# x and ctx transposed unscaled with 1/rms applied per K tile, column weights loaded in halves, first stage in a pinned order

## The chip, the cores and the metric

One core of one Trainium2 chip runs the kernel. The metric is device time in microseconds (us) of one execution. The kernel before takes 1290.29 us (median of three runs, 1290.16 to 1291.49).

## What is computed

One layer of a transformer block on 256 latent tokens (x) and 256 context tokens (ctx), model width 2048, everything in float32. The part that matters here is the beginning of it:

```
sh1, sc1 = first two of six parts of  silu(c) @ w_mod + b_mod          # for x
csh1, csc1 = the same of  silu(c_ctx) @ w_mod + b_mod                  # for ctx
h  = rmsnorm(x,   g_attn) * (1 + sc1)  + sh1
hc = rmsnorm(ctx, g_attn) * (1 + csc1) + csh1
cq, ckv, kr, qn, kn, vn, f = split(h @ w_in);  the same of hc @ w_in
```

Three head groups (latent attention, neighbourhood attention, Fourier mixing), an output projection, and a gated feed-forward with a convolution follow. rmsnorm divides each token's row by its root mean square (rms) and multiplies by a gain.

## The kernel before, in words

Every matrix product is made of three products in float32r: each operand is split into a high part (limb) H, its value rounded to float32r, and a low limb L, the rest. `mm3` (lines 107 to 114) issues H*H, H*L and L*H, which the profile shows as lines 108, 109 and 110. `split` makes limbs: a CAST on ACT (line 119) and a subtraction on DVE (line 120).

The weights come as one stream of tiles in a fixed list, `order`, of 1 MB each (`raw`, line 169), issued on SP's queue; `take` splits quarters of them into limbs (`hl`), four quarters ahead. A raw tile lies in a pool of 16 buffers of 8 KB per partition, which x, the transposed xT, the normed hx and hc and others share.

The first stage runs from the start of the program to about 145 us. Its steps:

- x and ctx come as four tiles `x` of 128 tokens (line 288). ACT squares and sums each (line 295), DVE and POOL make 1/rms (lines 104 and 105), and DVE multiplies the whole tile by it in place (line 297). Then PE transposes it in 16 pieces of 128 columns, four to a PSUM bank (line 360), and DVE and ACT in turn copy the banks to xT (line 361). PE's transposes use the unit matrix `ident`, which is the first part of the packed constants `sm`, loaded by ACT's queue (line 291).
- Then a loop over 16 K tiles (128 rows of w_in each) with three kinds of work on PE. A column sum, `mod1_mm`: 32 matmuls over two raw tiles of w_mod (line 314) that give the shift and scale of this K tile, copied to SBUF by ACT as `part` (line 317). `mod1_h`: two transposes of `part` (line 322), three small DVE operations to `mt` (lines 326 to 328), and the normed K tile in limbs: DVE makes it in full (line 338), ACT its high limb hx or hc (line 339), DVE the low one (line 340). And `g1`: seven column groups of w_in times this K tile, 42 matmuls per K tile, accumulated in seven PSUM banks `g`. Their weights are the raw tiles A, one for two K tiles, split in four quarters: quarters 0 and 1 belong to the even K tile, 2 and 3 to the odd one.

In the code the column sum of K tile g stands ahead of four products of K tile g-1, then `mod1_h` of g, then the other three products (`G1_CUT` is 4 of `N_A` = 7). A scheduler places the instructions of the five engines; each engine then works through its own list strictly in that order. After the loop the stage of the neighbourhood values (V) begins, and beside it columns of the late modulation parts are summed on DVE from tiles `wm`, loaded by POOL's queue (lines 217 and 232); their limbs `acl` are summed over partitions by PE (lines 266 and 267).

## Time and profile before

| what | value |
|---|---|
| median of three runs | 1290.29 us |
| span of the profiled execution | 1286.6 us |
| median less that span | 3.7 us |
| PE busy | 1251.4 us, 97% of the span |
| DVE busy | 982.8 us, 76% |
| ACT busy | 699.7 us, 54% |
| DMA, mean rate | 237 GB/s |
| end of the first stage (first product of V) | 144.92 us |

The span runs from the first to the last instruction; the 3.7 us are what the median of the runs has beside it (the profile gives no other time of its execution). Times below count from the span's start. PE is the engine that the kernel is built around: it has little idle time, so a stage is read by when PE begins, what it must do, and where it waits.

### The profile page before, as it was taken

The numbers are of one execution on the slowest core, as the hardware profiler recorded it, in microseconds if no ns is written. First come the engines' busy times: TensorE is split into PE (matmuls) and PEld (weight loads), VectorE is DVE, ScalarE is ACT, GpSimd is POOL, SyncE is SP. The second block draws the span as 40 slices with busy tenths as digits, with TensorE's granted clock in tenths as the row PEclk, the third lists the DMA queues.
The fourth block names the chain that finished last, engine by engine and source line by source line (L and its number), as shares of the span: only waits on it lengthen the run. The fifth ranks groups of instructions, "written<-read, shape, count | busy, mean of one in ns | idle before, by whom it ended". The sixth has DMA issues, their size and how long they took to land.

```text
span 1286.6 us, 22194 instructions
## 1 busy us (share of the span) xinstructions
PE 1251.4 (97%) x8688; PEld 1129.4 (88%) x8688; DVE 982.8 (76%) x1805; ACT 699.7 (54%) x1327; POOL 115.0 (9%) x177
## 2 busy tenths in 40 slices
PE   5999989999999999999999999999999999999996
PEld 4888869998887888999999788999988999899985
DVE  5444588999989788798988956778766778777785
ACT  5333323765555555576666544666654566456662
POOL 0000121111111013212111100000000000000000
PEclk9999989999999999999999999999999999999998
DMA  9998688776756977766666657544455645554521
GB/s 384 419 404 317 233 291 313 239 251 240 246 196 250 363 279 293 306 255 236 227 229 230 229 196 290 184 149 164 169 192 209 243 141 193 190 207 160 189 107 66
DMA packets 53657, 304.96 MB, mean 237 GB/s; under 512 B 6064, under 2 KB 7216, under 8 KB 26800
## 3 DMA queue, kind: packets, MB, share of 16 engines
q1 hardware_dynamic: 34256, 234.37, 48.8%
q0 software_dynamic: 18432, 67.12, 15.2%
q10 hardware_dynamic: 864, 2.05, 0.4%
q8 instruction: 68, 1.11, 0.3%
q14 instruction: 37, 0.30, 0.1%
HBM read 301.42 MB, written 2.10 MB: 236 GB/s over the span
## 4 chain that ended last, share of the span: by engine, by line
PE 92%; DMA 3%; DVE 2%; ACT 1%; issue 1%; POOL 0%; DVEq 0%; POOLq 0%; ACTq 0%
PE ps L108 27%; PE ps L110 26%; PE ps L109 26%; PE g L108 2%; PE ms L314 2%; DMA wm<-in_wm_dram 2%; PE g L109 2%; PE g L110 2%; PE ps L489 1%; PE ps L360 1%; DMA sm<-in_small_dram 1%; DVE acc L232 1%; DVE hl L120 1%; PE ps L256 1%; ACT hl L119 0%
## 5 line engine op out<-in xcount | busy, mean ns | idle before, releaser
L119 ACT CAST hl<-raw 128x512 fp32r<-128x512 f32 (+2 forms) x732 | 443.6, 610 | 397.6 <-PE ps L110 315.7
L120 DVE TENSOR_TENSOR hl<-raw,hl 128x512 fp32r<-128x512 f32 (+2 forms) x732 | 486.4, 676 | 161.1 <-ACT hl L119 155.7
L108 PE MATMUL ps<-h,hl 128*128 128x258 f32 x1408 | 398.5, 283 | 0.0
L109 PE MATMUL ps<-h,hl 128*128 128x258 f32 x1408 | 396.2, 281 | 0.0
L110 PE MATMUL ps<-h,hl 128*128 128x258 f32 x1408 | 395.8, 281 | 0.0
L109 PEld LDWEIGHTS ps<-h,hl 128*128 128x128 f32 x1408 | 266.5, 189 | 0.2
L110 PEld LDWEIGHTS ps<-h,hl 128*128 128x128 f32 x1408 | 265.8, 189 | 0.0
L108 PEld LDWEIGHTS ps<-h,hl 128*128 128x128 f32 x1408 | 265.4, 189 | 0.2
L232 DVE SCALAR_TENSOR_TENSOR acc<-wm,c,acc 128x1024 f32<-128x1024 f32 x120 | 153.3, 1277 | 8.4 <-DMA wm<-in_wm_dram 8.2
L108 PE MATMUL ps<-hl,act 128*128 128x512 f32 x344 | 135.1, 393 | 0.0
L109 PE MATMUL ps<-hl,act 128*128 128x512 f32 x344 | 135.0, 393 | 0.0
L110 PE MATMUL ps<-hl,act 128*128 128x512 f32 x344 | 134.8, 392 | 0.0
L217 POOL DMA_DIRECT2D wm<-in_wm_dram x128 | 68.3, 534 | 303.1 <-DVE acc L232 225.5
L110 PEld LDWEIGHTS ps<-hl,act 128*128 128x128 f32 x344 | 64.7, 188 | 14.6
L108 PEld LDWEIGHTS ps<-hl,act 128*128 128x128 f32 x344 | 64.6, 188 | 14.3
L109 PEld LDWEIGHTS ps<-hl,act 128*128 128x128 f32 x344 | 64.7, 188 | 14.1
L212 POOL COPY hold<-hl 128x1 f32<-128x1 f32 x36 | 37.3, 1037 | 278.0 <-DVE hl L120 275.5
L817 DVE SCALAR_TENSOR_TENSOR cv<-ps,sm,cv 128x255 f32<-128x255 f32 x88 | 42.1, 481 | 24.8 <-ACT cv L816 24.4
L105 POOL TENSOR_TENSOR r<-v,mhalf 128x1 f32<-128x1 f32 (+1 forms) x3 | 4.0, 1317 | 563.1 <-DVE v L104 563.1
L816 ACT ACTIVATE cv<-ps,sm 128x256 f32<-128x256 f32 x88 | 49.5, 566 | 2.6
L108 PE MATMUL ps<-hl,mix 128*128 128x512 f32 x128 | 50.5, 394 | 0.0
L109 PE MATMUL ps<-hl,mix 128*128 128x512 f32 x128 | 50.1, 391 | 0.0
(272 smaller groups left out, 1996.1 us busy)
## 6 DMA issues: line engine op xcount, KB each, us to landing
raw<-in_wup_dram SPq DMA_DIRECT2D x88, 1024.0 KB, 4.9
wm<-in_wm_dram POOLq DMA_DIRECT2D x128, 512.0 KB, 4.8
raw<-in_wdn_dram SPq DMA_DIRECT2D x44, 1024.0 KB, 4.8
raw<-in_wm_dram SPq DMA_DIRECT2D x32, 1024.0 KB, 14.5
raw<-in_wo_dram SPq DMA_DIRECT2D x16, 1024.0 KB, 8.3
raw<-in_wB_dram SPq DMA_DIRECT2D x10, 1024.0 KB, 7.9
raw<-in_wA_dram SPq DMA_DIRECT2D x8, 896.0 KB, 14.8
x<-in_x_dram SPq DMA_DIRECT2D x4, 1024.0 KB, 8.8
```

Of the source, the lines that this page charges most:

```text
L108: pe.matmul(ps, lH, rH, start=first, stop=False, skip_group_check=skip)
L109: pe.matmul(ps, lH, rL, start=False, stop=False, skip_group_check=skip)
L110: pe.matmul(ps, lL, rH, start=False, stop=last, skip_group_check=skip)
L119: act.copy(H, src)
L120: return dve.tensor_tensor(L, src, H.bitcast(F32), ALU.subtract).ins
L212: hold = pool.tensor_copy(tiny(1, "hold"), recent[0][:, 1, 0:1].bitcast(F32)).ins
L217: pool.dma_start(w, a["wm2"][blk * 16 + kt])
L232: dve.scalar_tensor_tensor(m2["a"], w, c1[:, kt : kt + 1], m2["a"], ALU.mult, ALU.add)
L256: pe.matmul(ps[:, 2 * j : 2 * j + 2], v[:, j * P : (j + 1) * P], ones[:, 0:2], start=True, stop=True)
L314: pe.matmul(ms[r : r + 32, 0:256], cs[:, 8 * q + k, :], w[:, k, :], start=(q == 0 and k < 4), stop=(q == 1 and k >= 4), tile_position=(0, r))
L816: act.activation(t, ps[:, :SEQ], AF.Identity, bias=c[:, 3:4], scale=c[:, 1:2])
L817: dve.scalar_tensor_tensor(t[:, 1:], ps[:, : SEQ - 1], c[:, 0:1], t[:, 1:], ALU.mult, ALU.add)
```

## The change

- x and ctx are loaded in halves of 1024 columns, and PE transposes them as they land, unscaled, with a unit matrix `idt` that POOL makes (so that it needn't wait for `sm`). DVE alone copies the banks. `sm` is issued behind them in the code, `rope` later.
- 1/rms of all 512 tokens is made at once; four diagonal blocks `dgx` of it and one matmul with ones spread it over the partitions (`rxb`), and DVE multiplies it into xT, 512 columns per K tile, one K tile ahead of use.
- Each A tile comes in halves of 448 KB (896 columns). The second half (quarters 2 and 3) is issued behind the next K tile's two raw tiles of w_mod.
- `G1_CUT` is 2, K tile 1 has an order of its own, and `tc.issue_after` holds the column sums and the transposes behind the last `g1` product issued ahead of them in the code, and the DVE multiplication behind the last one's h.

```diff
-N_A, G1_CUT = 7, 4
+N_A, G1_CUT = 7, 2
...
+    idt = const.tile([P, P], F32, name="idt")
+    pool.affine_select(idt, ones, [[1, P]], ALU.is_equal, 0.0, base=0, channel_multiplier=-1)
...
-            last_dma[0] = sync.dma_start(raw[:, :w], a[name][idx]).ins
+            if key[0] == "A":
+                sync.dma_start(raw[:, : w // 2], a[name][idx, :, : w // 2])
+                late_half.append((raw[:, w // 2 : w], a[name][idx, :, w // 2 :]))
+            else:
+                last_dma[0] = sync.dma_start(raw[:, :w], a[name][idx]).ins
+                if late_half and key[0] == "m" and key[2] == 1:
+                    sync.dma_start(*late_half.pop())
...
-        sync.dma_start(x_, (a["x"] if t < 2 else a["ctx"])[(t % 2) * P : (t % 2 + 1) * P, :])
+        for h in range(2):
+            sync.dma_start(x_[:, h * 1024 : (h + 1) * 1024],
+                           (a["x"] if t < 2 else a["ctx"])[(t % 2) * P : (t % 2 + 1) * P, h * 1024 : (h + 1) * 1024])
...
-        act.activation(junk, xt[t], AF.Square, accum_out=ssx[:, t : t + 1])
-        rstd(rx[:, t : t + 1], ssx[:, t : t + 1], D)
-        dve.tensor_scalar(xt[t], xt[t], rx[:, t : t + 1], None, ALU.mult)
...
+                pe.transpose(ps[:, k * P : (k + 1) * P], xt[t][:, kt * P : (kt + 1) * P], idt)
+            dve.tensor_copy(xT[m][:, :, t * P : (t + 1) * P], ps.rearrange("p (k q) -> p k q", k=4))
+    rstd(rx, ssx, D)
+    dgs = b2(s="dgx")
+    for t in range(4):
+        dve.tensor_scalar(dgs[:, t * P : (t + 1) * P], idt, rx[:, t : t + 1], None, ALU.mult)
+    ps = bank()
+    pe.matmul(ps, ones, dgs, start=True, stop=True)
+    rx_made = act.copy(rxb, ps).ins
...
+            if g:
+                held.enter_context(tc.issue_after(g1_last[-1]))
...
+            dve.tensor_tensor(xk, xk, rxb, ALU.mult)
...
+        if g == 1:
+            g1(0, range(0, 4))
+            sb = mod1_mm(1)
+            with tc.issue_after(rx_made):
+                act.dma_start(rope, a["rope"])
+                act.activation(c1, smv("c1"), AF.Silu)
+            g1(0, range(4, 5))
+            mod1_h(1, sb)
+            g1(0, range(5, N_A))
+            continue
```

PE's list at the start of the loop. `raw` are tiles of w_mod, `ms` the bank of the column sums, `part` the sums on their way to the transposes, `g` the products. Before:

```order
L314 MATMUL ms_118<-raw_222,cs 32x256 x8
L314 MATMUL ms_118<-raw_224,cs 32x256 x8
L322 MATMUL ms_118<-sm,part_254 128x128 x2
L314 MATMUL ms_118<-raw_228,cs 32x256 x8
L314 MATMUL ms_118<-raw_230,cs 32x256 x8
L322 MATMUL ms_118<-sm,part_294 128x128 x2
L314 MATMUL ms_118<-raw_232,cs 32x256 x8
L108 MATMUL g_0_34_215<-hx_262,hl_296 128x256
```

Two and a half column sums and two pairs of transposes stand ahead of the first product there. PE's list of the changed kernel, at the same place:

```order
L317 MATMUL ps_211<-dgx_206,ones_r 128x512
L338 MATMUL ms_214<-raw_222,cs 32x256 x8
L338 MATMUL ms_214<-raw_224,cs 32x256 x8
L349 MATMUL ms_214<-idt,part_255 128x128 x2
L110 MATMUL g_0_34_215<-hx_264,hl_274 128x256
L110 MATMUL g_1_35_216<-hx_264,hl_274 128x256
```

One column sum and one pair of transposes stand ahead of the first product now, and the matmul that spreads 1/rms stands ahead of all of them.

ACT's list at the same place. `raw_226` is the first A tile; `hl_296` to `hl_305` are its four quarters, `hx_262` and `hc_263` the high limbs of the first K tile. Before:

```order
L317 COPY part_254<-ms_118 128x256
L119 CAST hl_296<-raw_226 128x512
L119 CAST hl_299<-raw_226 128x384
L119 CAST hl_302<-raw_226 128x512
L119 CAST hl_305<-raw_226 128x384
L317 COPY part_294<-ms_118 128x256
L339 ACTIVATE hx_262<-xT_77,mt_258 128x256
L339 ACTIVATE hc_263<-xT_77,mt_258 128x256
```

In the changed kernel the same A tile is `raw_226`, quarters 0 and 1 of it are `hl_274` and `hl_277`, quarters 2 and 3, from the late half, `hl_280` and `hl_283`:

```order
L122 CAST hl_274<-raw_226 128x512
L122 CAST hl_277<-raw_226 128x384
L394 ACTIVATE c_77<-sm 128x16
L341 COPY part_255<-ms_214 128x256
L122 CAST hl_280<-raw_226 128x512
L122 CAST hl_283<-raw_226 128x384
L371 ACTIVATE hx_264<-xT_79,mt_259 128x256
L371 ACTIVATE hc_265<-xT_79,mt_259 128x256
```

The two casts of the late half still stand ahead of the first K tile's high limbs, while the tile that they read now comes in two transfers, the second behind two more raw tiles of w_mod.

ACT's list around K tiles 4 and 5 before (`part_636` is the sum of K tile 5, `hx_586` with `mt_582` the limb of K tile 4):

```order
L119 CAST hl_644<-raw_374 128x512
L317 COPY part_554<-ms_118 128x256
L119 CAST hl_647<-raw_374 128x384
L317 COPY part_636<-ms_118 128x256
L339 ACTIVATE hx_586<-xT_78,mt_582 128x256
L339 ACTIVATE hc_587<-xT_78,mt_582 128x256
```

The copy of the next K tile's sum stands ahead of this K tile's limbs there; the list before has this at K tiles 4, 8 and 12 alike. In the list of the changed kernel it stands so at K tile 12 alone (`part_1343` is the sum of K tile 13, `hx_1280` with `mt_1275` the limb of K tile 12):

```order
L341 COPY part_1259<-ms_214 128x256
L122 CAST hl_1351<-raw_1076 128x512
L122 CAST hl_1354<-raw_1076 128x384
L341 COPY part_1343<-ms_214 128x256
L371 ACTIVATE hx_1280<-xT_82,mt_1275 128x256
L371 ACTIVATE hc_1281<-xT_82,mt_1275 128x256
```

Two of the three places are gone. Behind the first stage the lists of all five engines are the same before and after.

## Rows read from the trace of the kernel before

**Rows 1.** Page: the span, and busy time, share and instructions of each engine.

```profile
span 1286.6 us, 22194 instructions
PE 1251.4 (97%) x8688; PEld 1129.4 (88%) x8688; DVE 982.8 (76%) x1805; ACT 699.7 (54%) x1327; POOL 115.0 (9%) x177
```

**Rows 2.** Windows: length, busy us (instructions) by engine, granted clock, DMA share, GB/s.

```profile
9.00:10.00 1.00, 0.00 (x0) 0.00 (x0) 0.00 (x0) 0.51 (x2) 0.00 (x0) 1.00 1.05 426
20.00:30.00 10.00, 8.15 (x104) 5.52 (x106) 7.49 (x18) 6.50 (x13) 0.00 (x0) 1.00 1.02 423
60.00:80.00 20.00, 19.93 (x198) 17.43 (x202) 8.66 (x27) 6.72 (x14) 0.00 (x0) 1.00 1.01 417
```

**Rows 3.** Timeline of SP's queue: start, us, line, output and input, count.

```profile
0.75 0.87 SPq L288 DMA_DIRECT2D x<-in_x_dram  x2
6.60 0.43 SPq L169 DMA_DIRECT2D raw<-in_wA_dram  x1
9.48 6.25 SPq L169 DMA_DIRECT2D raw<-in_wm_dram  x4
```

**Rows 4.** DMA issues from 6.5 to 7 and from 9 to 10 us: us to landing.

```profile
raw<-in_wA_dram SPq DMA_DIRECT2D x1, 896.0 KB, 15.5
...
raw<-in_wm_dram SPq DMA_DIRECT2D x1, 1024.0 KB, 15.1
```

**Rows 5.** Timeline of PE, 23 to 31 us, with idle time before and what ended it.

```profile
23.36 1.93 PE L314 MATMUL ms<-raw,cs 128*32 128x256 f32 x32
25.79 0.44 PE L322 MATMUL ms<-sm,part 128*128 128x128 f32 x2 [0.49 <-ACT part L317]
30.95 0.39 PE L108 MATMUL g<-hx,hl 128*128 128x256 f32 x1
```

**Rows 6.** Timeline of ACT, 25 to 30 us.

```profile
25.63 1.96 ACT L119 CAST hl<-raw 128x512 fp32r<-128x512 f32 x4
28.83 0.60 ACT L339 ACTIVATE hx<-xT,mt 128x256 fp32r<-128x256 f32 x1
```

**Rows 7.** Chain that ended last: column sums of K tiles 3, 7, 8, 9, 11 and 15.

```profile
42.52 1.86 PE ms L314 x32
72.67 1.86 PE ms L314 x32
79.91 1.86 PE ms L314 x32
87.15 1.91 PE ms L314 x32
102.89 1.86 PE ms L314 x32
132.75 1.86 PE ms L314 x32
```

**Rows 8.** Timeline of ACT at 89 us, with idle time before.

```profile
89.08 0.37 ACT L317 COPY part<-ms 128x256 f32<-128x256 f32 x1 [6.46 <-PE ms L314]
89.35 0.60 ACT L339 ACTIVATE hx<-xT,mt 128x256 fp32r<-128x256 f32 x1
```

**Rows 9.** Timeline of PE: first matmul of V, the two waits for acl.

```profile
144.92 0.39 PE L108 MATMUL ps<-hl,hx 128*128 128x512 f32 x1
183.46 0.80 PE L266 MATMUL ps<-acl,ones_r 128*128 128x512 f32 x1 [3.39 <-ACT acl L119]
730.05 0.51 PE L266 MATMUL ps<-acl,ones_r 128*128 128x512 f32 x1 [1.62 <-ACT acl L119]
```

**Rows 10.** Windows: granted clock (column before the last two) around the two waits.

```profile
182.00:184.00 2.00, 0.54 (x1) 0.29 (x1) 1.92 (x3) 1.22 (x3) 0.54 (x1) 0.66 0.95 365
186.00:188.00 2.00, 2.00 (x6) 1.55 (x5) 2.00 (x3) 0.00 (x0) 0.54 (x1) 0.50 0.60 178
188.00:190.00 2.00, 2.00 (x7) 1.52 (x7) 1.25 (x3) 0.62 (x1) 0.54 (x1) 0.63 0.63 234
190.00:192.00 2.00, 2.00 (x10) 1.65 (x9) 1.96 (x2) 0.19 (x1) 0.54 (x1) 1.00 0.70 234
728.00:730.00 2.00, 0.43 (x2) 0.00 (x0) 1.95 (x3) 0.63 (x2) 0.00 (x0) 1.00 0.00 0
```

**Rows 11.** Page: a costly group of DVE: busy, mean ns of one, idle before.

```profile
L120 DVE TENSOR_TENSOR hl<-raw,hl 128x512 fp32r<-128x512 f32 (+2 forms) x732 | 486.4, 676 | 161.1 <-ACT hl L119 155.7
```

More of the change, by code (lines that the diff above doesn't have):

```diff
@@ L109, in mm3 @@
         pe.matmul(ps, lH, rL, start=False, stop=False, skip_group_check=skip)
-        pe.matmul(ps, lL, rH, start=False, stop=last, skip_group_check=skip)
+        ins = pe.matmul(ps, lL, rH, start=False, stop=last, skip_group_check=skip).ins
         pace[1] += pace[0] * 3 * rH.shape[-1] * 0.427e-3
@@ L114, in mm3 @@
             fill()
+        return ins
     def split(H, L, src, scale=None):
@@ L141, in block_kernel @@
            "d": ("wdn", 2048)}
-    raws, hls = {}, {}
+    raws, hls, late_half = {}, {}, []
     recent, last_split, last_dma = [None], [None], [None]
@@ L287, in block_kernel @@
         x_ = b8([P, D], s="x")
-        sync.dma_start(x_, (a["x"] if t < 2 else a["ctx"])[(t % 2) * P : (t % 2 + 1) * P, :])
+        for h in range(2):
+            sync.dma_start(x_[:, h * 1024 : (h + 1) * 1024],
+                           (a["x"] if t < 2 else a["ctx"])[(t % 2) * P : (t % 2 + 1) * P, h * 1024 : (h + 1) * 1024])
         xt.append(x_)
-        if t == 0:
-            act.dma_start(sm, a["small"])
-    act.dma_start(rope, a["rope"])
+    act.dma_start(sm, a["small"])
+    rxb = b2(s="rxb")
     for t in range(4):
         junk = b8([P, D], s="junk")
-        act.activation(junk, xt[t], AF.Square, accum_out=ssx[:, t : t + 1])
-        rstd(rx[:, t : t + 1], ssx[:, t : t + 1], D)
-        dve.tensor_scalar(xt[t], xt[t], rx[:, t : t + 1], None, ALU.mult)
-    act.activation(c1, smv("c1"), AF.Silu)
+        sq_last = act.activation(junk, xt[t], AF.Square, accum_out=ssx[:, t : t + 1]).ins
+        for m in range(4):
+            ps = bank()
+            for k in range(4):
+                kt = 4 * m + k
+                pe.transpose(ps[:, k * P : (k + 1) * P], xt[t][:, kt * P : (kt + 1) * P], idt)
[4 more added lines that the diff above has]
+        dve.tensor_scalar(dgs[:, t * P : (t + 1) * P], idt, rx[:, t : t + 1], None, ALU.mult)
+    ps = bank()
+    pe.matmul(ps, ones, dgs, start=True, stop=True)
+    rx_made = act.copy(rxb, ps).ins
+    hmade, g1_last = [], []
     hx, hc = [None] * 4, [None] * 4
@@ L307, in mod1_mm @@
     def mod1_mm(g):
-        for q in range(2):
-            w = raw_tile(("m", g, q), 6)
-            w = w.rearrange("p (k n) -> p k n", k=8)
-            for k in range(8):
-                r = 32 * (k % 4)
-                pe.matmul(ms[r : r + 32, 0:256], cs[:, 8 * q + k, :], w[:, k, :], start=(q == 0 and k < 4),
-                          stop=(q == 1 and k >= 4), tile_position=(0, r))
+        with ExitStack() as held:
+            if g:
+                held.enter_context(tc.issue_after(g1_last[-1]))
+            for q in range(2):
+                w = raw_tile(("m", g, q), 6)
+                w = w.rearrange("p (k n) -> p k n", k=8)
+                for k in range(8):
+                    r = 32 * (k % 4)
+                    pe.matmul(ms[r : r + 32, 0:256], cs[:, 8 * q + k, :], w[:, k, :], start=(q == 0 and k < 4),
+                              stop=(q == 1 and k >= 4), tile_position=(0, r))
         sb = b1(s="part")
@@ L320, in mod1_h @@
     def mod1_h(kt, sb):
-        for s in range(2):
-            pe.transpose(ms[:, 256 + s * P : 256 + (s + 1) * P], sb[:, s * P : (s + 1) * P], ident)
+        with ExitStack() as held:
+            if kt:
+                held.enter_context(tc.issue_after(g1_last[-1]))
+            for s in range(2):
+                pe.transpose(ms[:, 256 + s * P : 256 + (s + 1) * P], sb[:, s * P : (s + 1) * P], idt)
         t = tiny(4, "mt")
@@ L329, in mod1_h @@
         m = kt // 4
+        xk = xT[m][:, kt % 4, :]
+        with ExitStack() as held:
+            if kt:
+                held.enter_context(tc.issue_after(hmade[-1]))
+            dve.tensor_tensor(xk, xk, rxb, ALU.mult)
         if hx[m] is None:
@@ L352, in g1 @@
             mm3(accs[i][:, :SEQ], lH, lL, *hsl(hx, kt), first=(kt == 0), last=(kt == KT - 1), skip=True)
-            mm3(accs[i][:, SEQ:], lH, lL, *hsl(hc, kt), first=False, last=(kt == KT - 1), skip=True)
-    for t in range(4):
-        for m in range(4):
-            ps = bank()
-            for k in range(4):
-                kt = 4 * m + k
-                pe.transpose(ps[:, k * P : (k + 1) * P], xt[t][:, kt * P : (kt + 1) * P], ident)
-            (act.copy if m % 2 else dve.tensor_copy)(xT[m][:, :, t * P : (t + 1) * P],
-                                                     ps.rearrange("p (k q) -> p k q", k=4))
+            g1_last.append(mm3(accs[i][:, SEQ:], lH, lL, *hsl(hc, kt), first=False, last=(kt == KT - 1), skip=True))
     accs = [bank(f"g1_{i}") for i in range(N_A)]
     for g in range(KT):
+        if g == 1:
[8 more added lines that the diff above has]
+            continue
         sb = mod1_mm(g)
```

2 lines of the change are left out of this document (1 added, 1 removed).

## The prediction

> **What bounds the kernel now.** I read the page first: PE is busy for 1251.4 of 1286.6 us [rows 1], so the time is what PE must do, plus the little it waits, plus when it begins. The change touches only the first stage, so the next views were of that stage. The windows show its DMA at a share of 1.01 to 1.05, some 420 GB/s, from the start to about 80 us [rows 2]: at first the loads set the pace. The timeline of PE shows when that ends: the first product of the loop comes at 30.95 us [rows 5], and from there PE is busy (19.93 of 20 us in the window from 60 us [rows 2]). The stage ends with the first matmul of V at 144.92 [rows 9]. So PE takes 144.92 - 30.95 = 114.0 us from the first product to the end of the stage, and this bounds the stage; the loads bound only what comes ahead of 30.95.
>
> The chain of waits shows how evenly the 114.0 us run. Column sums that follow each other undisturbed start 7.24 us apart (79.91 and 87.15 [rows 7]): one sum (1.86), one pair of transposes (0.44 [rows 5]) and 42 products. Four K tiles should take 28.96 us, but from 42.52 to 72.67 it is 30.15, from there to 102.89 it is 30.22, and to 132.75 it is 29.86 [rows 7]: 1.19, 1.26 and 0.90 too much, 3.35 together. The rows of ACT show why: the copy of the next sum stands ahead of this K tile's high limb on ACT and waits 6.46 us for PE, and the limb starts only behind it, at 89.35 [rows 8]; PE, which has by then run out of products, waits with it. That is the place of the lists at K tiles 4, 8 and 12.
>
> **The change, term by term.** All durations are from the profiled execution, span 1286.6; the median of the runs is 1290.29, so 3.7 lie outside the span, and I keep them.
>
> *When the first product can start.* The earlier transposes look like a gain of many us, since column sums began at 23.36 [rows 5] and depended on the scaling. But the first product needs the high limb of K tile 0 from ACT, and in the changed list ACT first casts the late half of the first A tile, which SP issues behind two more raw tiles of w_mod. When does it land? Before, the A tile was issued at 6.60 and landed 15.5 later, at 22.1; the raw tile behind it was issued at 9.48 and landed 15.1 later, at 24.6 [rows 3, 4]. So 1 MB takes 2.5 us of the stream. Ahead of the late half's end stands what stood ahead of 22.1, plus two raw tiles: 22.1 + 5.0 = 27.1. The 256 KB of `rope`, issued later now, may fall behind it, which takes off up to 0.6; I take 26.8. Then ACT needs two casts (half of 1.96, so 1.0) and the limb (0.60) [rows 6]: 28.4, and the first product at 28.5. Against 30.95 that is **-2.45** (bounds -2.75 and -2.15). Does something else end later? The second raw tile of w_mod lands 2.2 ahead of the A tile, at 19.3 without `rope`; a sum takes 1.93, or twice that at the low clock, the copy 0.4, the transposes 0.44 to 0.9, and the three small DVE operations some 0.6: 22.7 to 25.1. That is 2.7 us or more ahead of the 27.8 at which ACT is through with the casts. So the whole prologue (halves of x, unit matrix by POOL, one DVE copying instead of two engines, 1/rms at once, the spreading matmul) is covered by the late half, and gives and costs nothing; without that cover it would set the start.
>
> *What PE has done by then.* Before, 2.5 sums and two pairs of transposes were done at 30.95; now, by the list, one sum and one pair. PE has to make up 1.5 sums of 1.9 and one pair of 0.44 after its first product: **+3.3**. So the earlier start is more than paid back: PE stands idle, for want of the late half, while work that it used to do there waits behind the first product in its list.
>
> *The clock.* PE has nothing to do from the end of the transposes (22.7 to 25) to 28.5, 3.5 to 5.8 us. The nearest row is the wait of 3.39 us that ended at 183.46 [rows 9]: the granted clock fell to 0.50 in it, at 182.6 (0.66 over the window from 182 means 1.36 us of low clock) and came back at 189.5 (0.63 over the window from 188) [rows 10]. [...] A wait of 1.62 us left it at 1.00 [rows 9, 10]. The new gap is as long as the first one or longer, so I expect the low clock when the products begin, for 5 to 6 us: **+2.75** (bounds 0 and 3.4, half of the 6.8 us for which it was low there).
>
> *What the pinned order takes away.* All three late limbs are 3.35 us. In the changed list two are gone, the one at K tile 12 is left. **-3.35 and +1.2** (bounds of what is left: 0.90 and 1.26).
>
> *Edits at nothing.* The DVE multiplication of xT by 1/rms (512 columns; about 0.68 us, as the DVE subtractions over 512 columns take, most of whose group has that form [rows 11]) runs once per 7.24 us on a DVE that is busy 8.66 of 20 us [rows 2], and one K tile ahead of its use; if it came late it would hold the low limb by 0.7. With `G1_CUT` 2, five groups of products (3.5 us) and a sum (1.9) cover the way from the transposes to the next limbs, where three groups did before. The stage behind has the same lists on all engines, so a shift of the stage's end is carried to the end of the program one to one.
>
> The halves of A and x put four more transfers of x and one of A into SP's queue ahead of the late half. The rows show a queue that pays nothing per transfer: `sm`, x and w_mod of different sizes move at a share of 1.05 [rows 2]. The bounds are nothing and SP's own time per issue, 0.87 / 2 = 0.43 [rows 3], each, and I take nothing, since the transfers already queue ahead of their turn. [...]
>
> **Sum:** -2.45 + 3.3 + 2.75 - 3.35 + 1.2 = +1.45. Span 1288.05, and with 3.7 outside 1291.7.
>
> **Rivals.**
>
> *The clock does not fall, or is back when the products begin.* For it speaks that the record shows one fall only, in a wait for a DVE and ACT chain; against it that the new gap is longer. -2.75: 1289.0. [...]
>
> *The halves do cost queue time* (the one that ends slower). Place: SP's queue ahead of the late half. Price: five more transfers at up to 0.43 are 2.15, so the first product comes at 30.6 and the time is 1293.9. It decides from about 0.23 us per transfer on, where the sum passes +2.6. Against it: the share of 1.05.
>
> *The late half does not hold ACT.* If the first limb were not behind it, the limb would be ready at about 24.2, the gap would be under 2 us, and the sum would be -6.75 + 3.3 - 2.15 = -5.6: 1286.1. This is the change as it reads in words. The list of ACT speaks against it.
>
> *The wait at 183 shrinks.* The loads of `wm` and the weights of V share the queues there, and the stage's end moves against them. If the 3.39 us became the 1.62 of the second wait, the clock would stay up: -1.8 - 3.0 = -4.8, so 1286.9. Against it: everything in that stage starts from the same lists, relative to its own start.
>
> **How the numbers follow.** The forecast has 0.59 and, by its own bounds, 1290.0 to 1293.3; the clock rival 0.13, the queue 0.14, the late half that holds nobody 0.06, the shrinking wait 0.08. A measurement of this kernel can tell about 0.2% (2.6 us) from no change. Above 1292.9 lie the queue's 0.14 and 0.12 of the forecast: slower 0.26. Below 1287.7 lie the last two, 0.14. The rest, 0.60, is within 0.2%. For 8 in 10 the range leaves out the late-half rival, half of the shrinking wait and the upper half of the queue: 1287.0 to 1294.0.
>
> **What would show it.** In the profile after: transposes of x from about 5 us, with the first sum at 19 to 20; ACT waiting for a DMA of A ahead of its third cast, until 26.5 to 27.1; the first product at 28.5; a granted clock of 0.5 for some 5 us around 30; one limb late at K tile 12 and none at 4 and 8; V's first matmul at 146 to 147. A first product ahead of 26, or a full clock at 30, would make it wrong, and so would a second wait of PE in the loop that these lists don't show.

## The result, and the profile after

| | before | after |
|---|---|---|
| median of the runs beside each other | 1290.22 us (4 runs) | 1295.8 us (4 runs, 1294.8 to 1296.7) |
| ratio, 95% interval | | 1.0054 (1.0033 to 1.0074) |
| span of the profiled execution | 1286.6 us | 1293.5 us |
| first product of the loop | 30.95 | 30.30 |
| first matmul of V | 144.92 | 147.19 |

The changed kernel is slower by 5.6 us (by the medians), and 1295.8 lies above the range that was forecast, 1287.0 to 1294.0. In a second pair, side by side on one chip, the two stood at 1288.15 and 1298.11 (runs n_before and n_after below). The page of the kernel after, first lines, beside [rows 1]:

```profile
span 1293.5 us, 22221 instructions
PE 1263.5 (98%) x8690; PEld 1137.3 (88%) x8690; DVE 993.5 (77%) x1826; ACT 695.9 (54%) x1320; POOL 115.3 (9%) x175
```

PE is busy 12.1 us longer than before, for two records more. That is the first thing to see: the time didn't go into waits alone. The first stage first, by the steps of the prediction. SP's queue, beside [rows 3]:

```profile
0.80 2.12 SPq L298 DMA_DIRECT2D x<-in_x_dram  x4
2.96 3.24 SPq L298 DMA_DIRECT2D x<-in_ctx_dram  x4
7.39 0.85 SPq L176 DMA_DIRECT2D raw<-in_wm_dram  x2
8.86 0.33 SPq L173 DMA_DIRECT2D raw<-in_wA_dram  x1
10.12 2.94 SPq L176 DMA_DIRECT2D raw<-in_wm_dram  x2
13.95 0.33 SPq L178 DMA_DIRECT2D raw<-in_wA_dram  x1
```

The first A transfer goes out at 8.86, where it was 6.60 [rows 3]; eight transfers of x keep SP until 6.2 us, and w_mod starts at 7.39. The late half goes out at 13.95. ACT's timeline, beside [rows 6], shows when it was there:

```profile
28.71 1.03 ACT L122 CAST hl<-raw 128x512 fp32r<-128x512 f32 x2 [2.89 <-DMA raw<-in_wA_dram]
29.65 0.60 ACT L371 ACTIVATE hx<-xT,mt 128x256 fp32r<-128x256 f32 x1
```

ACT waits 2.89 us for the DMA until 28.71, and the high limb stands behind its two casts, as foreseen, but 1.9 us later than foreseen. Where the 1.9 us arose can be read from the landings: the first half of A, the late half and `rope`, issued at 8.86, 13.95 and 22.05, with the us from issue to landing in the last column:

```profile
raw<-in_wA_dram SPq DMA_DIRECT2D x1, 448.0 KB, 12.5
raw<-in_wA_dram SPq DMA_DIRECT2D x1, 448.0 KB, 14.7
rope<-in_rope_dram ACTq DMA_DIRECT2D x1, 256.0 KB, 7.4
```

The first half lands at 21.3, some 0.6 us later than the forecast's own figures put it (26.8 less 5.0 for two raw tiles and 1.1 for 448 KB). The late half lands 7.3 us behind it instead of 6.1. The forecast had let `rope` fall half behind the late half; it was under way beside it, and its 256 KB are 0.6 us of the stream by the same 2.5 us for 1 MB.

PE's timeline, beside [rows 5, 9]:

```profile
19.96 2.04 PE L317 MATMUL ps<-dgx,ones_r 128*128 128x512 f32 x2 [3.56 <-DVE dgx L315]
21.94 3.44 PE L338 MATMUL ms<-raw,cs 128*32 128x256 f32 x32
25.88 0.44 PE L349 MATMUL ms<-idt,part 128*128 128x128 f32 x2 [0.50 <-ACT part L341]
30.30 0.79 PE L110 MATMUL g<-hx,hl 128*128 128x256 f32 x2 [3.99 <-ACT hx L371]
147.19 0.39 PE L110 MATMUL ps<-hl,hx 128*128 128x512 f32 x1
185.12 0.52 PE L275 MATMUL ps<-acl,ones_r 128*128 128x512 f32 x1 [2.88 <-ACT acl L122]
733.17 0.50 PE L275 MATMUL ps<-acl,ones_r 128*128 128x512 f32 x1 [0.61 <-ACT acl L122]
```

PE waits 3.56 us for `dgx`, a wait that the prediction didn't name, and 3.99 us for hx. The first of the two doesn't hold the first product: DVE's last operation for `mt` is over at 26.98, and the limb's place on ACT, behind the casts of the late half, comes only at 29.65:

```profile
26.82 0.16 DVE L355 SCALAR_TENSOR_TENSOR mt<-mt,sa 128x2 f32<-128x2 f32 x1
```

The windows show what that did to the clock (columns: length, busy us and instructions by engine, granted clock, DMA share, GB/s), beside [rows 10]:

```profile
0.00:5.00 5.00, 0.00 (x0) 0.00 (x0) 0.67 (x3) 0.00 (x0) 0.48 (x5) 1.00 0.56 170
20.00:25.00 5.00, 5.00 (x34) 1.81 (x34) 1.76 (x3) 1.63 (x4) 0.00 (x0) 0.50 1.03 426
28.00:32.00 4.00, 1.70 (x7) 1.59 (x8) 2.19 (x5) 2.03 (x4) 0.00 (x0) 0.56 0.99 410
32.00:36.00 4.00, 4.00 (x27) 3.78 (x30) 0.34 (x1) 0.99 (x2) 0.00 (x0) 0.59 1.04 427
185.00:189.00 4.00, 3.68 (x9) 2.72 (x10) 3.92 (x8) 1.11 (x3) 0.76 (x2) 0.57 0.79 300
```

The granted clock is at 0.50 from 18.2 to 25.0 and from 28.4 to 35.3: the column sum takes 3.44 us instead of 1.93, and 18 of the first products, from 31.29 to 35.13, start 0.213 us apart, where 0.117 is the spacing at 1.00.

**Where the rest went.** How much later the same matmul comes than before, read from the two timelines of PE: -0.65 at the first product, +2.27 at V, +0.78 at 198 us, +1.08 at 222, +1.58 at 381, +2.92 at 559, +5.23 at 986, +7.30 at the last one of the down projection (1275.7 and 1283.0). So 1.5 us of V's shift are gone by 198 us, and from there to the end 6.5 us arise, steadily, where the lists of all engines are the same and no wait is new. The second wait for `acl` even gives 1.0 us back on the way: it is 0.61 us long in after and was 1.62 [rows 9], and the shift goes from +4.13 ahead of it to +3.13 behind it. Windows in the middle of the up and the down projection; before:

```profile
570.00:670.00 100.00, 100.00 (x836) 99.83 (x836) 90.09 (x178) 65.09 (x125) 19.37 (x26) 1.00 0.66 235
954.00:1000.00 46.00, 46.00 (x202) 37.67 (x202) 29.66 (x46) 20.58 (x34) 0.00 (x0) 1.00 0.59 215
```

and after:

```profile
570.00:670.00 100.00, 100.00 (x831) 99.83 (x830) 89.51 (x174) 64.77 (x126) 19.49 (x25) 1.00 0.64 229
954.00:1000.00 46.00, 46.00 (x200) 37.26 (x199) 29.26 (x45) 20.59 (x34) 0.00 (x0) 1.00 0.54 193
```

PE is busy throughout at a granted clock of 1.00 in both, and does 831 matmuls where it did 836. As a number for this I take the *spacing*: the mean time from the start of a matmul to the start of the next of the same product, from the records of the trace, without the steps that have a wait or other work between them. In the up projection (4224 matmuls of 258 columns) it is 119.40 ns before and 120.27 after; in the down projection (1032 of 512) 230.13 and 231.9; in the output projection (384) 228.1 and 231.8; in the first stage's products 116.9 and 117.8. 4224 x 0.87 + 1032 x 1.8 + 384 x 3.7 = 3.7 + 1.9 + 1.4 = 7.0 us. That accounts for most of the 7.5 us that came up behind 198 us, the 6.5 that are left and the 1.0 that the second wait gave back.

### The profile page after: what moved, and what is told of

Its sections match the earlier page's. It is cut to its first block, busy times and chain, and to the rows that moved or that the text cites. A ratio compares the mean times of both kernels' runs of the same rounds, so it can differ in the third digit from the quotient of the medians.

```text
span 1293.5 us, 22221 instructions
## 1 busy us (share of the span) xinstructions
PE 1263.5 (98%) x8690; PEld 1137.3 (88%) x8690; DVE 993.5 (77%) x1826; ACT 695.9 (54%) x1320; POOL 115.3 (9%) x175
## 4 chain that ended last, share of the span: by engine, by line
PE 92%; DMA 4%; DVE 1%; ACT 1%; issue 1%; POOL 0%; DVEq 0%; POOLq 0%; ACTq 0%
PE ps L110 27%; PE ps L112 27%; PE ps L111 27%; DMA wm<-in_wm_dram 2%; PE g L110 2%; PE ms L338 2%; PE g L111 2%; PE g L112 2%; DMA raw<-in_wA_dram 1%; PE ps L523 1%; DMA x<-in_ctx_dram 1%; DVE acc L241 1%; PE ps L265 1%; DMA sa<-in_small_a_dram 0%; PE ms L349 0%
```

## Experiments: the spacing

What differs behind the first stage, if not the lists? The chip, the addresses of the pools in SBUF, which of the sixteen 8-KiB buffers (tag `b8`) and which PSUM bank each tile gets, and PE's list, which has one float32 matmul more at the start. The pools hand out a buffer in the order in which buffers came back, and the changed first stage gives them back in another order, so that from `hx` on every tile of before has another buffer in after, one to one (5 is 2 there, 8 is 3, and so on). They stand 8256 bytes apart.

**n_before and n_after**: the two kernels unchanged, on one chip.

> The kernel before, unchanged. In the two profiles so far the first stage ends 2.27 us later after the change, but the last matmul comes 7.3 us later: from 228 to 1262 us the shift grows from 1.16 to 7.28, with equal lists and no new waits, since matmuls of the up projection follow each other in 120.55 ns instead of 119.72 (mean). Theory of the chip: the two profiles fell on chips or moments of different speed; then this one shows about 120.5 like the changed kernel in the same job, and the true difference of the kernels is some 1 us. Theory of the addresses: the changed kernel's tiles lie elsewhere in SBUF and PE reads them slower; then this one shows 119.7 again, and a ratio of 1.000.

> The changed kernel, unchanged, beside n_before on the same chip. Theory of the addresses: 120.5 ns and 5 to 6 us slower than before. Theory of the chip: the same spacing as n_before and about 1 us slower.

1288.15 and 1298.11 us, ratio 1.0074 (1.0053 to 1.0094); spacing 119.40 and 120.27 ns in the up projection, 230.1 and 231.9 in the down projection, as in the first pair to 0.1 ns. Not the chip, then: the spacing belongs to the kernel.

**b_both and a_lay**: the pools' addresses exchanged, by a constant and a small buffer that nobody reads, and in the kernel after by putting the unit matrix in `rope`'s place.

```
b_both:  +    idt = const.tile([P, P], F32, name="idt")        # and: early = b2(s="early")
a_lay:   -    idt = const.tile([P, P], F32, name="idt")
         +    idt = rope[:, 0, 0:P]
```

> The kernel before with its tiles moved in SBUF alone: a 512-byte constant that nobody reads, and the pool of b2 opened early by a tile that nobody reads, so that every pool lies at the byte addresses it has in the changed kernel (hl from 203040 instead of 192288, cv from 188192 instead of 216864; the 16 large buffers 512 bytes further, dealt out as before). First stage as before. Theory of the addresses: up to 6 us slower than before, spacing towards 120.5. Theory of the chip: as n_before.

> The changed kernel with its pools at the byte addresses of the kernel before: the unit matrix lies in the buffer of rope, whose load is issued behind the first stage, and the pools are opened in the old order by tiles that nobody reads. The 16 large buffers are still dealt out as in the changed kernel. Theory of the addresses: spacing back towards 119.7, and 0 to 3 us slower than before (the first stage's 2.3 and the wait in V, 1.3 shorter, remain). Theory of the chip: as n_after.

b_both 119.40 and 230.12 ns, 1288.28 us (1.0002); a_lay 120.27 and 232.0 ns, 1295.01 us (1.0052). The pools' addresses don't matter either; in both, the sixteen were still dealt out as in the kernel that each came from.

**s_slots, s_banks, s_pe, a_back**: the three that are left, one at a time from before, and the way back from after. Buffers are dealt out otherwise by taking all sixteen at the start and giving them back in a chosen order:

```
s_slots: +    hold8 = [b8([P, D], s="hold8") for _ in range(16)]
         +    for i in (*range(16), *(1, 10, 15, 3, 4, 0, 9, 2, 5, 6, 7, 8, 14, 13, 12, 11)):
         +        dve.memset(hold8[i][:, 0:1], 0.0)
s_banks: the same with eight banks;  a_back: after, both, back to the places of before
s_pe:    +    pe.matmul(ms, ones, xt[0][:, 0:512], start=True, stop=True)
```

> The kernel before, whose sixteen 8-KiB buffers are written and given back at the start in such an order that every later tile lies where the kernel after has it; PSUM banks and PE's list are those of before. It computes the same. The matmuls of the up projection follow each other in 119.4 ns in before and in 120.27 ns in after. Theory of the buffers (it matters in which of the 8-KiB buffers h, h2 and the weights lie): 120.2 ns here, 231.9 ns in the down projection, and about 6 us more than before, near 1295. Theories of the PSUM banks and of PE's list: 119.4 and 230.1 ns, and a time within 0.3% of before, the small writes at the start (about 2 us of DVE) lying ahead of the first data.

> The kernel before, whose eight PSUM banks are written and given back at the start in such an order that every later product gathers in the bank that it has in the kernel after; buffers in SBUF and PE's list are those of before. It computes the same. Theory of the banks: 120.2 ns between matmuls of the up projection, 231.9 ns in the down projection, near 1295 us. Theories of the buffers and of PE's list: 119.4 and 230.1 ns, and a time within 0.3% of before.

> The kernel before with one more float32 product of 512 columns (the size of the one that spreads 1/rms in the kernel after) into a bank whose content is not read, between the transposes of x and the column sums: two more matmul records and two more weight loads ahead of all the rest, as in after; buffers and banks as in before. It computes the same. Theory of PE's list (where its instructions lie in memory as they are fetched): 120.2 ns between matmuls of the up projection, 231.9 ns in the down projection, near 1295 us. Theories of the buffers and of the banks: 119.4 and 230.1 ns, and before plus at most 2 us for the product itself.

> The kernel after, whose sixteen 8-KiB buffers and eight PSUM banks are written and given back at the start in such an order that every later tile lies where the kernel before has it; PE's list is that of after. It computes the same. If buffers or banks make the slower spacing: 119.4 ns in the up projection, 230.1 ns in the down projection, and only the first stage's part of the difference left, that is before plus 1 to 3 us, near 1291. If PE's list makes it: 120.27 and 231.9 ns, and the time of after, 1295 to 1298, plus up to 2 us for the writes at the start.

The window from 570 to 670 us of s_slots, s_banks and a_back, in this order:

```profile
570.00:670.00 100.00, 100.00 (x830) 99.83 (x829) 89.91 (x176) 64.09 (x123) 19.40 (x24) 1.00 0.63 227
```

```profile
570.00:670.00 100.00, 100.00 (x836) 99.83 (x836) 90.05 (x176) 65.45 (x126) 18.84 (x24) 1.00 0.68 240
```

```profile
570.00:670.00 100.00, 100.00 (x836) 99.83 (x836) 90.12 (x176) 65.21 (x125) 19.12 (x25) 1.00 0.67 236
```

s_slots takes on the spacing of after (120.27 and 232.0 ns; 1297.66 us, with V at 150.00, 5.1 us later than in before, since its first stage runs otherwise), s_banks keeps that of before (119.40, 230.1; 1290.65), and a_back, which is the changed kernel in the buffers of before, has the spacing of before: 119.40 and 230.1 ns, 1289.73 us, 1.0012 of before (0.9999 to 1.0025). So the buffers make the difference, and the change itself, without them, costs some 1.5 us, which can't be told from nothing. s_pe tells nothing: its matmul reads x longer, so the buffers came back in another order there too, and it has spacings of its own (119.21, 231.6; 1293.0). That PE's list doesn't matter follows from a_back.

**p32, p96, p64**: what of a buffer matters? All sixteen are made 8320 bytes (65 x 128) apart, so that all begin at one place within 128 bytes; small pads shift them against the start of the weights' limbs (`hl`, whose six tiles stand 4096 apart).

```
         -        return sp.tile(shape, dt, tag="b8", bufs=16, name=nm(s))
         +        t = sp.tile([P, 2080], dt, tag="b8", bufs=16, name=nm(s))    # cut and shaped to `shape`
p96:     +    dve.memset(sp.tile([P, 16], F32, tag="lo", bufs=1, name="lo"), 0.0)    # 64 bytes ahead of the sixteen
p64:     p96 and 64 bytes more between the sixteen and hl (the small buffers beside hl move with it)
```

> The kernel before with its sixteen buffers 8320 instead of 8256 bytes apart, so that all of them begin 32 bytes behind a multiple of 128; the tiles lie in the same of the sixteen as before, and the weights' limbs too begin 32 bytes behind a multiple of 128, as before. It computes the same. Theory of the phase (what matters of a buffer is where it begins within 128 bytes: in after all four buffers of h2 begin at 32, in before three of four at 96, and the product that reads h or h2 as its moving side takes 117 ns a matmul at 96 and 118.4 at 32 in the first stage of both): spacing 120.3 ns in the up projection, 231.9 ns in the down projection, 118.4 ns in the first stage, 1295 us. Theory that it is which buffers are near to each other or to what a DMA writes: spacings of before, 119.4, 230.1 and 116.8 ns, and 1288 us.

> The same as p32 but for 64 bytes: all sixteen buffers begin 96 bytes behind a multiple of 128. It computes the same. Theory of the phase: 118.6 to 118.9 ns in the up projection (the mean of the three buffers of h2 that begin there in before), 229.5 ns or less in the down projection, 117.0 ns in the first stage, and with 4224 matmuls of the up projection 0.6 ns shorter and 1032 of the down projection 0.8 ns shorter some 3 us less than before, 1285. Theory of the neighbours: spacings of before and 1288 us, and the same as p32.

> p96 with the weights' limbs 64 bytes further on: the sixteen buffers begin where they do in p96, 96 bytes behind a multiple of 128, but their distances from the limbs are those of p32 (a multiple of 128). It computes the same. Theory of the place: all spacings as in p96 (119.34 ns in the up projection, 117.5 ns in the first stage, V 232.7 ns, down projection 231.16). Theory of the distance between what a matmul reads as its moving side and what is loaded as weights beside it: all spacings as in p32 (120.04, 119.5, V 228.9 and 227.3 ns, down projection 231.01), and some 4 us more than p96, 1293.

| spacing, ns | p32 | p96 | p64 |
|---|---|---|---|
| up projection | 120.04 | 119.34 | 120.03 |
| down projection | 231.01 | 231.16 | 231.02 |
| products of the first stage | 119.5 | 117.5 | 119.5 |
| V, context tokens | 227.3 | 233.1 | 227.4 |
| time, us | 1294.28 | 1289.35 | 1294.52 |

The window from 570 to 670 us of p96 and p64, in this order:

```profile
570.00:670.00 100.00, 100.00 (x837) 99.83 (x836) 90.10 (x177) 65.45 (x126) 18.84 (x24) 1.00 0.66 237
```

```profile
570.00:670.00 100.00, 100.00 (x832) 99.82 (x831) 89.68 (x174) 64.94 (x124) 20.53 (x25) 1.00 0.65 230
```

As far as the place within 128 bytes goes, the theory failed in half of its numbers (p96 was to reach 118.6 to 118.9 and 229.5). But p64, whose buffers begin where they begin in p96, has the spacings of p32 to 0.1 ns, with which it shares the distance from the limbs and not the place. So it is the distance between the two operands. For a buffer that is loaded as weights while limbs stream (down projection; start of the buffer minus start of the limbs, modulo 256 bytes), one table then orders the tiles of all kernels, with some overlap:

| distance | 0 | 64 | 128 | 192 |
|---|---|---|---|---|
| spacing, ns | 226.7 to 228.0 | 233.1 to 233.4 | 232.1 to 233.4 | 228.9 to 230.3 (single tiles of after, s_slots and p96: 231.1 to 232.3) |
| of the eleven tiles of `act`, before | 3 | none | 4 | 4 |
| the same, after | none | 5 | 2 | 4 |

So it happened that before had three tiles of `act` at the best distance and none at 64, and after none at the best and five at 64. For a buffer that streams (up projection) the same distance doesn't give one spacing: 118.4 to 121.1 at 0, 118.4 to 120.0 at 64, 119.2 to 119.3 at 192 and 120.3 to 121.2 at 128, so something beside this distance matters there, and 3.7 of the 7.0 us lie there.

**tuned**: the kernel before, with twelve of the sixteen dealt out by these tables (as in s_slots, x's loads ahead of the writes).

> The kernel before with the sixteen buffers dealt out by a table of distances taken from all runs so far (start of the buffer minus start of the limbs, modulo 256: as weights, 227.6 ns at 0, 229.3 at 192, 232.7 at 128 and 233.2 at 64; as the moving side of the up projection, modulo 1024: 118.4 at 0, 118.3 to 119.4 at 64, 118.6 at 576, 118.6 to 119.9 at 832, 120 to 121 at 128, 512, 640, 896). The four buffers of h2 go to 832, 576, 64 and 0, the eleven of act to 0 five times, 192 five times and 64 once; x's loads come ahead of the writes that deal out the other twelve. It computes the same. Theory of the distance: 118.5 ns in the up projection (119.40 in before) and 228.9 ns in the down projection (230.1), so 3.8 + 1.2 = 5.0 us less there, 0.4 us more in the first stage, 1283.5 to 1284.5 against 1288 of before. Theory of the place alone, or of chance: within 0.1% of before.

```profile
570.00:670.00 100.00, 100.00 (x838) 99.83 (x837) 89.88 (x175) 65.23 (x125) 18.85 (x24) 1.00 0.67 243
```

228.46 ns in the down projection (228.9 expected, 230.1 before), 119.18 in the up projection (118.5 expected, 119.40 before), 1286.01 us: 0.9970 of before (0.9952 to 0.9988). It beats both kernels, before by 2.3 us as the medians go and by 3.9 as the ratio goes, where 5 were expected. What failed is the table for the streaming side, which had been read buffer by buffer: three of the four buffers of h2 have 119.4 to 119.5 ns, where 118.5 was expected of the four.

## Experiments: the first stage

All of these stand on a_back, so that the spacing is out of the way; what is read is when V begins.

**f_whole** (the first A tile in one piece again), **f_warm** (seven products that nobody reads, in PE's two gaps), **f_all** (both, with five).

```
f_whole: -            if key[0] == "A":
         +            if key[0] == "A" and key[1]:
f_warm, which also holds the first column sum behind the product that spreads 1/rms:
         +    for _ in range(3):
         +        pe.matmul(ps, ones, sm[:, 0:512], start=True, stop=True)      # ahead of the spreading of 1/rms
         +                for _ in range(4):
         +                    pe.matmul(accs[6], ones, sm[:, 0:512], start=True, stop=True)   # behind part's transposes
```

> a_back with the first weight tile A loaded in one piece, ahead of the next column weights, as the kernel before loads it; the other A tiles in halves. It computes the same. By my step on ACT (the first h waits behind the limbs of the late half, whose data landed at 29.2 us in a_back, and was ready for 27): the limbs of A are made by 26, the first product starts near 28 instead of 30.8, and V's first matmul comes 2 us earlier than in a_back (147.0), at 145. Rival: the stage behind is bound by the column weights' landing, which come later by what the late half weighs (0.6 us), and V starts at 147 or later however early the first product is.

> a_back with seven float32 products of 512 columns that nobody reads, three between the last transposes and the product that spreads 1/rms, four between the transposes of the first column sums and the first product of A, in stretches in which PE waits in a_back (3.3 and 4.6 us). It computes the same. By my step on the clock (PE idles, the granted clock falls to half, and the column sum at 22.8 and the first products behind 30.8 run at half speed): the granted clock stays at 1.00 from 18 to 36 us, the column sum takes 1.9 us instead of 2.5, the first fifteen products 1.8 instead of 3.4, and V starts 1.5 to 2.3 us earlier than in a_back (147.0), at 145. Rival: the products only wait longer for data behind the first K tiles, and V's start stays within 0.5 us.

> f_whole and f_warm together, on a_back: the first A in one piece, three unread products ahead of the spreading of 1/rms and two between the first column sums' transposes and the first product. It computes the same. By my steps: first product near 28.5 to 29 us, no fall of the granted clock from 18 to 36 us, so the stage from first product to V's first matmul 115.5 us as in f_warm, and V at 144.2, 2.5 us earlier than in either of the two alone (146.7). Rival: what binds is the landing of the column weights, so that waits for data take the place of what is saved, and V stays at 146 or later.

**f_nohalf** and **f_nohw**: all A tiles in one piece, without and with the five products.

> a_back with every A tile loaded in one piece again, as the kernel before does; order pins, transposes of unscaled x and the product that spreads 1/rms stay. Five of the sixteen buffers are dealt out otherwise behind it, h2 lies as in before. It computes the same. Theory of the halves (a late half lands behind the next column weights, its limbs stand on ACT ahead of the copy of the next column sums, and PE's list waits there): first product at 28.8 us as in f_whole, no wait of PE for the copy of the column sums between 35 and 45 us, V at 145.5 or earlier. Rival (the landing of the column weights binds, halves or not): V at 146.5 or later.

> f_nohalf with the five unread products of f_all. It computes the same. Theory of the halves: no low granted clock from 18 to 36 us, first product at 26.4 to 28.8 us, stage from there 115.5 us, V at 144.3 or earlier, and some 1 us less than before, 1287. Rival (landing of the data): V at 146 or later, as f_all (147.2).

| | first product | low clock, 18 to 36 us | V's first matmul | time, us |
|---|---|---|---|---|
| a_back | 30.82 | 6.8 us | 147.02 | 1289.73 |
| f_whole | 28.77 | 10.2 us | 146.68 | 1289.24 |
| f_warm | 31.17 | none | 146.68 | 1290.37 |
| f_all | 26.40 | none | 147.23 | 1290.42 |
| f_nohalf | 28.28 | 10.2 us | 146.96 | 1290.4 |
| f_nohw | 27.28 | 3.4 us | 147.27 | 1292.06 |

Each row is one profiled execution, and V's start differs between two executions of one kernel too, by 0.3 us (before 144.92, n_before 145.22) and 0.2 us (after 147.19, n_after 146.96, although the clock was low for 6.8 us twice in the one and for 3.4 us twice in the other). So differences of 0.3 us in V tell nothing here; that the 2 us that were expected don't come does. The first product moves by 4.8 us and V by 0.6, in no order with it. Where the lead went shows when the starts of the same products are set against a_back's (us, minus is earlier; the times are a_back's):

| product | 1st, 30.82 | 3rd, 31.43 | 25th, 37.30 | 33rd, 38.57 | 43rd, 41.70 | 61st, 44.61 | V, 147.02 |
|---|---|---|---|---|---|---|---|
| f_whole | -2.06 | -1.31 | -0.10 | -0.11 | -0.12 | -0.33 | -0.34 |
| f_warm | +0.35 | +0.35 | -0.86 | -0.86 | -0.86 | -0.49 | -0.34 |
| f_all | -4.42 | -2.38 | -3.59 | -0.74 | +0.66 | +0.19 | +0.21 |
| f_nohalf | -2.54 | -1.79 | -0.90 | +0.28 | +0.27 | -0.20 | -0.06 |
| f_nohw | -3.54 | -1.50 | -1.18 | +0.59 | +0.58 | +0.11 | +0.25 |

All is over by 45 us; from there to V the five run alike. f_all has most to give back, and its timeline of PE, and behind it ACT's, shows to whom:

```profile
26.40 0.51 PE L116 MATMUL g<-hx,hl 128*128 128x256 f32 x2 [0.20 <-ACT hx L382]
29.06 0.39 PE L117 MATMUL g<-hx,hl 128*128 128x256 f32 x1 [2.15 <-DVE hx L383]
...
37.19 0.44 PE L356 MATMUL ms<-idt,part 128*128 128x128 f32 x2 [2.51 <-ACT part L348]
```

```profile
35.84 1.03 ACT L128 CAST hl<-raw 128x512 fp32r<-128x512 f32 x2 [9.00 <-DMA raw<-in_wA_dram]
36.77 0.36 ACT L348 COPY part<-ms 128x256 f32<-128x256 f32 x1
```

First PE waits 2.15 us for the low limb of K tile 0. Then it waits 2.51 us for the copy of the next column sums, which stands on ACT behind the limbs of the second A tile, and ACT has waited 9.00 us for that tile's data: 2.85 us of the lead are gone between the 25th and the 33rd product. Just behind that wait the granted clock falls (low for 3.4 us from 37.5), and 1.4 more are gone by the 43rd. The casts of the second A tile start at 35.01 in after, at 36.77 in f_nohw, whose A tiles are whole, and at 35.54 in before: the stream of loads, at 418 GB/s from 20 to 40 us in f_all, brings it at 35 to 37 us, halved or not. In f_whole the lead goes otherwise: 0.75 to the low limb, and 1.2 to the clock, which is low from 28.8 to 35.6 there and from 30.7 to 34.1 in a_back. Holding the clock alone (f_warm) does bring 1.2 us by the 25th product, and 0.37 of them go again at 43 us, to the copy behind the second half of the same tile.

So the theory of f_all fell: the steps are there, but neither is worth its length, since the second A tile's data come at 35 to 37 us, and in f_all the clock went low for 3.4 us just behind the wait of 2.51 us that they caused. Its rival had V right (146 or later) and named the wrong data, the column weights. I had also expected the halves to hold the stage (V at 145.5 and 144.3 without them), and that fell outright: f_nohalf and f_nohw are where f_whole and f_all are.

One run that was made for another purpose does have the second A tile earlier: a_lay, in which `rope`'s load is issued behind the whole first stage. Its ACT, and behind it that of n_after on the same chip:

```profile
27.34 1.03 ACT L122 CAST hl<-raw 128x512 fp32r<-128x512 f32 x2 [2.92 <-DMA raw<-in_wA_dram]
34.49 1.03 ACT L122 CAST hl<-raw 128x512 fp32r<-128x512 f32 x2 [5.13 <-DMA raw<-in_wA_dram]
```

```profile
28.13 1.03 ACT L122 CAST hl<-raw 128x512 fp32r<-128x512 f32 x2 [3.58 <-DMA raw<-in_wA_dram]
35.72 1.03 ACT L122 CAST hl<-raw 128x512 fp32r<-128x512 f32 x2 [5.57 <-DMA raw<-in_wA_dram]
```

The late half is there 0.8 us earlier and the second A tile 1.2, the first product comes at 28.92 (29.71 in n_after) and V at 145.98 (146.96). That is the earliest V of all kernels with the change, by 0.7 us, and but for that load the lists are those of after, and the spacing too. It is one execution, and the pools lie elsewhere in it, so it supports the reading without proving it.

## Why the prediction was wrong

**The step that failed** is the last sentence of *Edits at nothing*: "The stage behind has the same lists on all engines, so a shift of the stage's end is carried to the end of the program one to one." The lists are the same, but the tiles lie elsewhere, and the spacing of PE's matmuls went with that: 119.40 ns in the up projection and 230.1 in the down projection with the buffers of before (before, a_back), 120.27 and 231.9 to 232.0 with those of after (after, s_slots). It was priced at nothing and cost 6.5 us in the profiled execution, from 198 us to the end. With the buffers of before (a_back) the changed kernel takes 1289.73 us, which lies in the range. Nothing in the profile of before priced it; that the spacing within before goes from 228.0 to 232.7 ns, by buffer, was there to be read in the starts of the matmuls, and the changed order of release too.

The first stage came out near the forecast, +2.27 us at V instead of +1.45 (+1.74 in the second pair), but that is luck: an error of +1.8 us in the first term below and one of -1.25 in the next two cancel for the most part.

- *When the first product can start*: mis-sized, -0.65 instead of -2.45. The path is as described (late half, two casts, limb), and the late half did cover the prologue, but it was cast from 28.71 instead of 26.8. Some 0.6 us of that were there when the first half landed, and SP's queue is a likely cause: the first A transfer goes out 2.26 us later than before. The other 1.2 came between the two halves, where `rope`'s 0.6 us, which the forecast had taken half off, moved along; a_lay, without `rope` there, has 6.1 us between the halves. So the rival "the halves do cost queue time" has the number (30.6 for the first product, 30.30 measured, 29.71 in n_after), but only part of the reason. The prediction read the DMA's share as full from the start and took from it that a queue pays nothing per transfer. The windows of [rows 2] begin at 9 us; in the first 5 us, where most of the transfers of x are issued, the share is 0.56 and 170 GB/s, and 0.64 and 197 before.
- *What PE has done by then* and *the pinned order*: +3.3 and -3.35 + 1.2. Measured from start to start, waits included, between the first product and V: the column sums take 29.02 us instead of 27.34 and the transposes 2.04 instead of 3.82. One and a half sums and a pair more are thus paid for by the waits that are gone; one wait of 0.99 us is left, at 122.5 us. Net -0.1 instead of +1.15.
- *The clock*: as forecast behind the first product. It is low for 4.97 us there, some 2.2 us lost (18 products at 0.213 us each from 31.29 to 35.13, where 0.117 is the spacing at 1.00, are 1.7 of it), 2.75 foreseen. The products take 85.84 us instead of 82.82 on the way to V, 3.0 more: that is the clock's 2.2 and some 0.6 of their own wider spacing (672 x 0.9 ns). A first fall at 18.2, in the wait of 3.56 us for `dgx`, was not foreseen; it falls ahead of the first product and costs nothing there.
- That the length of each of these terms is its price at the stage's end: not so. Taking the clock's fall away moved V by 0.34 us (f_warm), the earlier first product by 0.34 (f_whole), both together by nothing (f_all), all three about as much as executions of one kernel differ, since what comes earlier meets the second A tile's landing.
- *The wait at 183*: 2.88 us instead of 3.39, and the clock low for 3.4 us instead of 6.8, so 1.5 us of V's shift were gone by 198 us. That is between the forecast and the rival "the wait shrinks", whose 3.0 us are half of the 6.0 from 183.46 [rows 9] to 189.5, where the clock was back at 1.00 [rows 10]; it can't be put down to the change, since n_before has 3.4 us and n_after 6.8 there.

The 3.7 us outside the span did not hold either: 1.7 us lay outside the profiled span of after (1295.24 and 1293.5), and 1.8 outside that of n_before (1286.2 and 1284.4); the rest of the 3.7 is how the profiled execution stands to the median.

Two sums of the prediction don't come out. The rival of the late half that does not hold ACT would be 1290.3 - 5.6 = 1284.7; 1286.1 took the 5.6 us from the forecast instead of from before. And the bounds of the terms add up to 1288.4 to 1292.8, where the forecast's own bounds are given as 1290.0 to 1293.3. The 1295.8 lie outside either way.

**Left open**: by which path the distance of the two operands makes a matmul start later. The runs show that it does and by how much, not the mechanism; and for the side that streams they don't give a rule that foretells the spacing. Nor was a first stage tried in the buffers of before that brings the second A tile earlier, which is what the table of V's starts and a_lay ask for.

## What to carry to other kernels

A change that alters the order in which buffers come back changes where every later tile lies, and here that alone cost more than what the change was about (6.5 us behind 198 us, against the 1.5 of a_back, which can't be told from nothing): compare the spacing of matmuls in a stage that the change doesn't touch before explaining the stage that it does. To separate the two, deal the buffers out as before at the start of the changed kernel, and measure that. An earlier start of the stage, or a clock that stayed up, was worth here only what the next load that landed late allowed: first products from 26.40 to 31.17 us gave V's from 146.68 to 147.27. So follow the list on past the first product to the next wait for a DMA.

## What the runs showed of the hardware

All figures here were measured in the runs of this case, and hold for them. Matmuls that follow each other without a wait, at a granted clock of 1.00, didn't follow at one rate: 226.7 to 233.4 ns for 512 columns and 118.4 to 121.2 for 258, tile by tile. For those of 512 columns the spacing went with the distance in SBUF, modulo 256 bytes, between what streams and the tile that is loaded as weights: 226.7 to 228.0 ns at 0, 228.9 to 230.3 at 192 (single tiles 231.1 to 232.3), 232.1 to 233.4 at 128 and 233.1 to 233.4 at 64. Shifting the limbs and the small buffers beside them by 64 bytes, with all else the same, moved V's from 233.1 to 227.4 ns (p96, p64); by what path is not shown. The means of the up and down projections repeat to 0.1 ns from run to run of one arrangement: 119.40 and 230.1 in before, n_before, b_both, s_banks and a_back, 120.27 and 231.9 to 232.0 in after, n_after, a_lay and s_slots.

The granted clock fell in a_back's waits of 3.26 and 4.63 us in the first stage, and not in f_warm's of 1.08 and 2.38; but it fell in or just behind waits of 2.24 us in f_whole and f_nohalf, and in f_nohw it was low from 30.0, behind a wait of 2.15. At the waits for `acl` at 183 to 188 us it didn't fall in b_both (a wait of 2.55 us), and where it fell, how long it stayed down, 3.4 or 6.8 us, differed from one execution of the same kernel to the next (before 6.8, n_before 3.4; after 3.4, n_after 6.8).
